# A decoder trunk on one core: query projection in 12 tiles instead of 16, with the rotary parts moved by DMA, and another order in front of the scan

## Chip, cores, metric

The kernel runs on one core of a Trainium2 chip. The metric is the device time of one execution in microseconds (us); lower is better. The engines are named as in the profile: PE (TensorE matrix products; PEld are its weight loads), DVE (VectorE), ACT (ScalarE), POOL (GpSimd), SP (SyncE, which issues most DMAs).

## What is computed

Two layers on 512 positions of width 1024, all in float32. Each layer has a mixer with two parallel head groups, then cross-attention into 256 memory tokens, then a gated MLP with a short convolution. The change is in the mixer:

```python
h = rmsnorm(x, norm_mix[i])
proj = h @ w_in[i]
z, xbc, dt_raw, c_q, c_kv, k_rope = jnp.split(proj, IN_SPLITS, axis=-1)
...
y = ssd_scan(xs, dt, a, bm, cm) + xs * d_skip[i][:, None]
...
q = (rmsnorm(c_q, q_norm) @ w_uq).reshape(b, s, MLA_HEADS, QK_NOPE + QK_ROPE)
q_nope = q[..., :QK_NOPE]
q_pe = apply_rope(q[..., QK_NOPE:], cos[:, :, None, :], sin[:, :, None, :])
kv = (rmsnorm(c_kv, kv_norm) @ w_ukv).reshape(b, s, MLA_HEADS, QK_NOPE + V_DIM)
...
k_pe = apply_rope(k_rope, cos, sin)
...
    sc = (jnp.einsum('bqhd,bkhd->bhqk', q_nope[:, q0:kend], k_nope[:, :kend])
          + jnp.einsum('bqhr,bkr->bhqk', q_pe[:, q0:kend], k_pe[:, :kend]))
```

There are 16 attention heads with 64 plain (nope) and 32 rotary (rope) query rows each; the query latent c_q has 384 channels, the key and value latent c_kv 256. The scan has 16 heads of 64 in 4 groups and runs over 4 chunks of 128 positions. `apply_rope` rotates pairs of rows by an angle that grows with the position.

## The kernel before

All matrices lie transposed: channels on the 128 partitions, the 512 positions along the free dimension. Every float32 product is made from three matmuls on values split into a high and a low part (`mm3`, L168 hi x hi, L169 hi x lo, L170 lo x hi). A result is split by `split`: ACT copies the high part (L159), DVE subtracts it for the low part (L162); with a scale it is L164 and L165. Weights come by DMA from SP into one of two raw buffers (L99, `fetch`), ACT makes the high part (L107) and POOL the low part (L108), each in three buffers; `weights` keeps two weights ahead. A raw buffer is free again when POOL has made the low part.

The order on PE is that of the program text (a manual schedule for PE alone). The other engines' instructions are put in order by a tile scheduler; each engine then runs its list strictly in order. `new("ps", ...)` takes one of 8 PSUM banks, `unit()` one of 68 SBUF tiles of 128x512.

A layer's mixer begins with the projections of the latents (`latent_q` three, `latent_kv` two), a projection that holds dt and the rotary keys, and the softplus chain for dt (L415 to L430). Then one loop runs the remaining projections (`inproj`, four groups of six tiles, each 24 matmuls of 128x512; four of a group pass a convolution over 4 positions on ACT and DVE: L485 scales the projection, L492, three times L494, a tanh in L495, the gate L496), and between the projections it hangs pieces of other work: the generator `front` from the first position on, and the four scans `ssd(g)` from the positions in START. Each `yield` gives way to the next projection:

```python
START = (5, 10, 16, 21)
...
for pos, _ in enumerate(chain(projections(), attention())):
    next(lead, None)
    ...
    for g in range(NG):
        if pos >= START[g]:
            next(scans[g], None)
```

`front` does, one piece at each position: the reciprocal root mean squares of the query latent (rq) and of the key latent (rk, and in layer 0 the rope tables, and the rotated keys kpe L440 to L443); the broadcast of rq and its products with the rope tables, csqa and csqb (L446, L447); the broadcast of rk and the normalised key latent (L452 and splits); the cumulative sums of dt x a by two matmuls (L460, L461) with acs, nacs, dtd and cd taken from them (L462 to L467); and the transposition of acs on PE (L470), which goes to DRAM and comes back broadcast (R in `ssd`).

A scan step `ssd(g)` transposes x, B and C pieces on PE (L515 to L522), makes xd = x dt and xdd = x dtd on DVE (L527, L536), exponentials on ACT (L543, L553) and their product with B x C on DVE (L554); after one more projection PE makes the states from xdd (L562), and later the outputs.

Attention goes head by head, in 16 steps. What a step holds is in strings: S scores of this head (`scores`: four blocks, on DVE a maximum L692, on ACT the exponential L695, the scale on POOL L697), K the keys of the next pair, V values, A outputs of two heads before (`attend`, L728 to L738), M one memory key tile (256 columns) in eight of the steps, T transposes of the head before (L709 and splits), Q the queries of two heads on (`queries`, L666):

```python
ORDER, FIRST, LAST = "SKVAMTQ", "VSKAMTQ", "SMAT"
```

A query tile is one head: 64 nope rows, 32 rope rows and the same 32 rope rows swapped, so that one multiplication with csqa (or csqb for odd heads, L666) gives the rotation's two products side by side; their sum is made inside the score product, since the keys hold kpe twice. 96 columns of weights thus cost a tile of 128, 16 tiles of nine matmuls per layer.

## Time and profile before

| | us |
|---|---|
| median of 3 runs | 1904.8 (1904.75 to 1904.96) |
| the profiled execution | 1904.88 |
| its span, from first to last instruction | 1903.2 |
| PE busy | 1867.0 (98%) |
| DVE, ACT, POOL busy | 1035.5, 950.2, 885.7 |
| granted clock of PE, mean | 0.995 |

Busy time is what an engine spends in instructions; idle time of an engine matters only where PE waits for it. The view of PE's waits sums such time by what ended it. The granted clock is given as a share of full speed: 1.0 is the 2.4 GHz level, 0.5 the 1.2 GHz level. Layer 0's front part runs from about 45 to 110 us and its attention from about 245 to 390 us; layer 1's from about 1000 and 1180 us.

### The profile page before, as it was taken

The page shows a single profiled execution, that of the slowest core. Times are in us where ns is not written, and L with a number is a line of the kernel's source. Part 1 is how long each engine was busy: PE and PEld are TensorE (multiplying, and loading weights), DVE is VectorE, ACT ScalarE, POOL GpSimd, SP SyncE. Part 2 cuts the span into 40 slices and gives each one's busy share as a digit, 9 for nine tenths or more (in the row PEclk, how much of TensorE's full clock was granted, in tenths as well). Part 3 has the DMA queues.
Part 4 walks back from the last instruction along what each step waited for, and adds up shares of the span by engine and source line. Part 5 has one row for each costly group of instructions (what it writes and reads, how often), then busy time and mean ns, then how long its engine had stood idle before and what let it go on. Part 6 is the DMA issues. An engine that isn't in the chain of part 4 may idle for free.

```text
span 1903.2 us, 24916 instructions
## 1 busy us (share of the span) xinstructions
PE 1867.0 (98%) x9264; PEld 1572.9 (83%) x9264; DVE 1035.5 (54%) x1967; ACT 950.2 (50%) x1694; POOL 885.7 (47%) x563
## 2 busy tenths in 40 slices
PE   8799999999999999999999999999999999999998
PEld 6588889988888888888887888898888888888887
DVE  5867788843343555541138777887334445555312
ACT  5366588843345444433235557888334544444321
POOL 5345455655416444433354454555553354444232
PEclk9899999999999999999999999999999999999999
DMA  5233311232213322233223332113322122332322
GB/s 168 68 122 111 103 51 59 93 125 94 91 34 109 100 100 97 92 97 100 92 100 101 113 110 82 58 62 122 110 91 88 50 96 98 100 100 90 102 91 84
DMA packets 56025, 178.47 MB, mean 94 GB/s; under 512 B 6368, under 2 KB 9312, under 8 KB 55904
## 3 DMA queue, kind: packets, MB, share of 16 engines
q1 hardware_dynamic: 49984, 166.32, 26.4%
q10 hardware_dynamic: 5920, 10.55, 1.7%
q8 instruction: 73, 1.20, 0.3%
q14 instruction: 48, 0.39, 0.1%
HBM read 174.69 MB, written 2.16 MB: 93 GB/s over the span
## 4 chain that ended last, share of the span: by engine, by line
PE 93%; DVE 2%; issue 1%; ACT 1%; POOL 1%; DMA 1%; SPq 0%; POOLq 0%; DVEq 0%; ACTq 0%
PE ps L168 28%; PE ps L170 28%; PE ps L169 28%; PE ps L728 2%; PE ps L709 1%; PE ps L583 1%; POOL wlo L108 1%; PE ps L589 1%; PE ps L562 1%; ACT whi L107 0%; DVE u L162 0%; PE ps L932 0%; PE ps L519 0%; PE ps L515 0%; PE ps L731 0%
## 5 line engine op out<-in xcount | busy, mean ns | idle before, releaser
L108 POOL TENSOR_TENSOR wlo<-wraw,whi 128x1024 fp32r<-128x1024 f32 (+1 forms) x290 | 679.1, 2343 | 855.7 <-ACT whi L107 836.6
L168 PE MATMUL ps<-u,whi 128*128 128x512 f32 (+1 forms) x2326 | 898.7, 386 | 7.7 <-ACT whi L107 5.1
L170 PE MATMUL ps<-u,wlo 128*128 128x512 f32 (+1 forms) x2326 | 890.0, 383 | 0.8 <-POOL wlo L108 0.6
L169 PE MATMUL ps<-u,whi 128*128 128x512 f32 (+1 forms) x2326 | 889.7, 383 | 0.0
L107 ACT ACTIVATE whi<-wraw 128x1024 fp32r<-128x1024 f32 (+2 forms) x319 | 328.2, 1030 | 494.7 <-PE ps L169 391.3
L168 PEld LDWEIGHTS ps<-u,whi 128*128 128x128 f32 x2326 | 438.9, 189 | 90.8 <-ACT whi L107 5.1
L170 PEld LDWEIGHTS ps<-u,wlo 128*128 128x128 f32 x2326 | 438.7, 189 | 87.3 <-POOL wlo L108 1.4
L169 PEld LDWEIGHTS ps<-u,whi 128*128 128x128 f32 x2326 | 439.2, 189 | 82.0 <-DVE u L165 0.7
L162 DVE TENSOR_TENSOR u<-ps,u 128x512 fp32r<-128x512 f32 (+2 forms) x236 | 137.2, 612 | 105.4 <-ACT u L159 104.7
L159 ACT ACTIVATE u<-ps 128x512 fp32r<-128x512 f32 (+2 forms) x236 | 117.7, 540 | 120.7 <-DVE ps L1021 98.4
L1017 DVE SCALAR_TENSOR_TENSOR u<-ps,small,u 128x510 f32<-128x510 f32 (+1 forms) x176 | 131.3, 749 | 74.7 <-ACT u L1015 71.7
L1010 DVE TENSOR_TENSOR ps<-ps,u 128x512 f32<-128x512 f32 x88 | 61.4, 700 | 109.9 <-PE ps L170 101.6
L301 POOL TENSOR_TENSOR u<-u,u 128x512 f32<-128x512 f32 (+1 forms) x82 | 102.5, 1251 | 37.0 <-ACT u L300 29.5
L108 DVE TENSOR_TENSOR wlo<-wraw,whi 128x1024 fp32r<-128x1024 f32 (+1 forms) x29 | 32.5, 1119 | 139.5 <-ACT whi L107 139.5
L697 POOL TENSOR_SCALAR u<-u,rs 128x512 f32<-128x512 f32 (+3 forms) x128 | 66.8, 537 | 79.7 <-DVE rs L696 75.0
L849 DVE TENSOR_TENSOR ps<-ps,u 128x512 f32<-128x512 f32 x32 | 22.4, 699 | 99.1 <-PE ps L170 99.1
L695 ACT ACTIVATE u<-ps,nm 128x512 f32<-128x512 f32 (+3 forms) x128 | 66.3, 524 | 18.1 <-DVE nm L692 12.1
L168 PE MATMUL ps<-u,u 128*128 128x512 f32 (+1 forms) x224 | 73.1, 326 | 0.9 <-ACT u L695 0.9
L170 PE MATMUL ps<-u,u 128*128 128x512 f32 (+1 forms) x224 | 72.1, 322 | 0.0
L169 PE MATMUL ps<-u,u 128*128 128x512 f32 (+1 forms) x224 | 72.0, 321 | 0.0
L494 DVE SCALAR_TENSOR_TENSOR u<-ps,half,u 128x509 f32<-128x509 f32 (+2 forms) x96 | 70.4, 742 | 1.2 <-ACT u L492 0.7
L1015 ACT ACTIVATE u<-ps,small 128x512 f32<-128x512 f32 x88 | 66.7, 760 | 1.7 <-DVE ps L1010 1.5
(193 smaller groups left out, 1769.3 us busy)
## 6 DMA issues: line engine op xcount, KB each, us to landing
wraw<-in_w_up SPq DMA_DIRECT2D x88, 512.0 KB, 3.4
wraw<-in_w_in SPq DMA_DIRECT2D x59, 512.0 KB, 3.5
wraw<-in_w_out SPq DMA_DIRECT2D x32, 512.0 KB, 3.4
wraw<-in_w_down SPq DMA_DIRECT2D x32, 512.0 KB, 3.4
u<-scr ACTq DMA_DIRECT2D x32, 256.0 KB, 4.6
wraw<-in_w_mk SPq DMA_DIRECT2D x16, 512.0 KB, 3.4
wraw<-in_w_mv SPq DMA_DIRECT2D x16, 512.0 KB, 3.4
wraw<-in_w_mq SPq DMA_DIRECT2D x16, 512.0 KB, 3.4
```

The lines of the kernel that those rows point to most:

```text
L107: A.activation(hi[:, c], raw[:, c], AF.Copy)
L108: eng.tensor_tensor(lo[:, c], raw[:, c], hi[:, c].bitcast(F32), ALU.subtract)
L159: A.activation(hi, src, AF.Copy)
L162: (leng or V).tensor_tensor(lo, src, hi.bitcast(F32), ALU.subtract)
L168: T.matmul(o, lh, rh, start=start, stop=False)
L169: T.matmul(o, lh, rl, start=False, stop=False)
L170: T.matmul(o, ll, rh, start=False, stop=stop)
L301: (eng or G).tensor_tensor(self.acc, self.acc, sq, ALU.add)
L494: V.scalar_tensor_tensor(r_[:, d:], acc[:, :S - d], cw(3 - d), r_[:, d:], ALU.mult, ALU.add)
L697: G.tensor_scalar(p_[:, :n], p_[:, :n], rs[:, i:i + 1], 1.0, ALU.mult, ALU.mult)
L1015: A.activation(y, acc, AF.Identity, scale=fw(2), bias=par(layer, "ffn_b", ch))
L1017: V.scalar_tensor_tensor(y[:, d:], acc[:, :S - d], fw(2 - d), y[:, d:], ALU.mult, ALU.add)
```

## The change

The weights of the queries are packed in 12 tiles per layer: four hold the rope rows of four heads each (`query_rope`), eight the nope rows of two heads each (`query_pair`). A rope tile is multiplied with the sine and with the cosine table into two banks, and both are split. The split rope rows (32 each) are then moved by DMA from SP into the query tiles of the heads, beside their nope rows: two products, high and low, two heads, so eight DMAs of 32x512 (64 KB) for each pair. The table of signs goes from the queries to the keys (`kro`, `krs`). The query latent is no longer multiplied in the query tile: `latent_q` keeps a copy, and `front` normalises and splits it (L482, L166 of the changed kernel).

In a step of attention the queries stand ahead of outputs and transposes, at the steps in UQ_AT. In `front`, the cumulative sums come one position earlier than the broadcasts; the rope tables and kpe follow behind the transposition of acs, then the key latent, then the query latent. The key tiles are filled one group later. The change's line numbers are those of the changed kernel, four to fourteen higher for the same statement in this part (L508 for L494, L499 for L485, L474 for L452, L541 for L527, L550 for L536, L576 for L562, L166 for L162).

```diff
+UQ = (-1, 0, 1, -1, 2, 3, -1, 4, 5, -1, 6, 7)
...
-    ORDER, FIRST, LAST = "SKVAMTQ", "VSKAMTQ", "SMAT"
+    ORDER, FIRST, LAST = "SKVMQAT", "VSKMQAT", "SMAT"
+    UQ_AT = (0, 1, 2, 4, 5, 6, 8, 9, 10, 12)
...
-        for nm, i, n in (("w_uv", 0, 1024), ("w_uk", 0, 1024), ("w_uq", 0, 768)):
+        for nm, i, n in (("w_uq", 0, 768), ("w_uv", 0, 1024), ("w_uk", 0, 1024)):
...
-            h_, l_ = unit(F32R), unit(F32R)
-            split(h_, l_, acc, par(layer, "q_norm", i))
+            r_ = unit()
+            A.copy(r_, acc)
             cqs.add(acc)
...
             rk = rstd_cols(cks.acc, KVL, rx)
-            if layer == 0:
-                rope_tables()
...
-            pq = bcast(rq)
-            V.tensor_tensor(csqa, pq, csa, ALU.mult)
-            V.tensor_tensor(csqb, pq, csb, ALU.mult)
-            yield
-            pk = bcast(rk)
...
+            yield
+            yield
             yield
 
             pa = bank()
...
             A.dma_start(scr, acsT)
+            yield
+
+            if layer == 0:
+                rope_tables()
...
+            kro, krs, ksh = unit(), unit(), unit()
...
+            yield
+            pk = bcast(rk)
...
+            yield
+            pq = bcast(rq)
+            for i in range(3):
+                V.scalar_tensor_tensor(cqr[i], cqr[i], par(layer, "q_norm", i), pq, ALU.mult, ALU.mult)
+                h_, l_ = unit(F32R), unit(F32R)
+                split(h_, l_, cqr[i])
...
+        def query_rope(i):
+
+            acc, sn = query_tile(i), bank()
+            V.tensor_tensor(sn, acc, css, ALU.mult)
+            V.tensor_tensor(acc, acc, csc, ALU.mult)
+            qpe[0] = []
+            for src in (acc, sn):
+                h_, l_ = unit(F32R), unit(F32R)
+                split(h_, l_, src)
+                qpe[0].append((h_, l_))
+
+        def query_pair(i, pr):
+
+            acc = query_tile(i)
+            for j in range(2):
+                qh, ql = unit(F32R), unit(F32R)
+                rows, r0, s0 = slice(64 * j, 64 * j + 64), 64 - 64 * j, 32 * ((2 * pr + j) % 4)
+                A.activation(qh[rows], acc[rows], AF.Copy)
+                V.tensor_tensor(ql[rows], acc[rows], qh[rows].bitcast(F32), ALU.subtract)
+                for c in range(2):
+                    for dst, src in zip((qh, ql), qpe[0][c]):
+                        nc.sync.dma_start(dst[r0 + 32 * c:r0 + 32 * c + 32].bitcast(F32),
+                                          src[s0:s0 + 32].bitcast(F32))
+                qq[2 * pr + j] = qh, ql
...
-                if g == 0:
+                if g == 1:
                     key_tiles()
```

Three places show how the order moves. **First place:** DVE around the products of the first scan step. In layer 0 before, ps_841 and ps_842 are the transposed x, u_866 and u_867 its xdd, ps_915 is the projection that PE finishes just ahead of the states matmul L562:

```order
L485 TENSOR_TENSOR ps_808<-ps_808,u_387 128x512
L527 TENSOR_TENSOR u_860<-ps_841,dt_151 128x512
L527 TENSOR_TENSOR u_862<-ps_842,dt_151 128x512
L494 SCALAR_TENSOR_TENSOR u_833<-ps_808,half,u_833 128x511
L536 TENSOR_TENSOR u_866<-ps_841,dtd_154 128x256
L494 SCALAR_TENSOR_TENSOR u_833<-ps_808,half,u_833 128x510
L536 TENSOR_TENSOR u_866<-ps_841,dtd_154 128x256
L494 SCALAR_TENSOR_TENSOR u_833<-ps_808,half,u_833 128x509
L536 TENSOR_TENSOR u_867<-ps_842,dtd_154 128x256
L485 TENSOR_TENSOR ps_915<-ps_915,u_387 128x512
```

In layer 0 of the change, ps_888 is the projection that PE finishes one broadcast (ps_921, of rq) ahead of the states matmul L576. The list begins

```order
L499 TENSOR_TENSOR ps_888<-ps_888,u_381 128x512
L482 SCALAR_TENSOR_TENSOR u_202<-u_202,small,ps_921 128x512
L482 SCALAR_TENSOR_TENSOR u_264<-u_264,small,ps_921 128x512
L474 SCALAR_TENSOR_TENSOR u_802<-u_336,small,ps_797 128x512
L508 SCALAR_TENSOR_TENSOR u_789<-ps_764,half,u_789 128x511
L482 SCALAR_TENSOR_TENSOR u_300<-u_300,small,ps_921 128x512
```

and after four more rows (L508, L166, L508, L474) ends with the gate, a low part, the products xd and, as u_839 and u_840, xdd:

```order
L510 SCALAR_TENSOR_TENSOR u_789<-ps_764,u_789 128x512
L166 TENSOR_TENSOR u_811<-u_808,u_810 128x512
L541 TENSOR_TENSOR u_833<-ps_814,dt_153 128x512
L541 TENSOR_TENSOR u_835<-ps_815,dt_153 128x512
L550 TENSOR_TENSOR u_839<-ps_814,dtd_156 128x256 x2
L550 TENSOR_TENSOR u_840<-ps_815,dtd_156 128x256
```

In layer 1 of the change (u_9131, u_9132 are xdd, ps_9180 is the projection ahead of the states matmul):

```order
L541 TENSOR_TENSOR u_9127<-ps_9107,dt_8499 128x512
L550 TENSOR_TENSOR u_9131<-ps_9106,dtd_8502 128x256 x2
L550 TENSOR_TENSOR u_9132<-ps_9107,dtd_8502 128x256
L499 TENSOR_TENSOR ps_9180<-ps_9180,u_8690 128x512
L482 SCALAR_TENSOR_TENSOR u_8538<-u_8538,small,ps_9213 128x512
```

The scaling of the projection ahead of the states matmul stood behind the three xdd before and does so in layer 1 of the change; in layer 0 of the change it stands ahead of them, with normalisations and splits between.

**Second place:** DVE in layer 0 around acs, before:

```order
L485 TENSOR_TENSOR ps_666<-ps_666,u_387 128x512
L162 TENSOR_TENSOR u_657<-u_654,u_656 128x512
L462 COPY acs_152<-ps_699 128x64
L463 TENSOR_SCALAR nacs_153<-ps_699 128x64
L494 SCALAR_TENSOR_TENSOR u_691<-ps_666,half,u_691 128x511
```

and of the change, where ps_609 is the projection just ahead of the two matmuls that fill ps_642:

```order
L510 SCALAR_TENSOR_TENSOR u_595<-ps_570,u_595 128x512
L499 TENSOR_TENSOR ps_609<-ps_609,u_381 128x512
L442 COPY acs_154<-ps_642 128x64
L443 TENSOR_SCALAR nacs_155<-ps_642 128x64
L444 TENSOR_TENSOR dtd_156<-ps_642,acs_154 128x64
```

The rows of the rope tables, of kpe, csqa and csqb and of the key latent that stood ahead of acs now stand behind it.

**Third place:** SP in layer 0's attention (u_2872 to u_2877 are split rope rows, u_2981 to u_2990 the query tiles of a pair). Before there were only weights:

```order
L99 DMA wraw_2961<-in_w_mk 128x1024
L99 DMA wraw_3022<-in_w_uq 128x768
L99 DMA wraw_3053<-in_w_mk 128x1024
L99 DMA wraw_3212<-in_w_uq 128x768
L99 DMA wraw_3298<-in_w_mk 128x1024
```

and of the change:

```order
L103 DMA wraw_3212<-in_w_uq 128x768
L704 DMA u_2981<-u_2872 32x512
L704 DMA u_2982<-u_2873 32x512
L704 DMA u_2981<-u_2876 32x512
L704 DMA u_2982<-u_2877 32x512
L704 DMA u_2989<-u_2872 32x512
L704 DMA u_2990<-u_2873 32x512
L704 DMA u_2989<-u_2876 32x512
L704 DMA u_2990<-u_2877 32x512
L103 DMA wraw_3333<-in_w_mk 128x1024
```

The eight DMAs of a pair stand between weight loads, behind one that waits for its raw buffer. On PE, 8780 rows become 8708; on SP, 332 become 456.

## Rows read from the trace of the kernel before

**Rows 1.** The page, part 1: busy us (share of the span), instructions.
```profile
PE 1867.0 (98%) x9264; PEld 1572.9 (83%) x9264; DVE 1035.5 (54%) x1967; ACT 950.2 (50%) x1694; POOL 885.7 (47%) x563
```

**Rows 2.** PE's waits: us in total, times, longest us.
```profile
PE ps L470 <- DVE acs L462: 10.7, 1, 10.7
PE ps L282 <- DVE rstd L275: 5.4, 2, 2.9
...
PE ps L168 <- ACT u L695: 1.9, 4, 0.5
```

**Rows 3.** PE's timeline in the fronts: start us, us, instruction [idle before <-releaser].
```profile
88.19 0.42 PE L470 MATMUL ps<-ident,acs 128*64 128x128 f32 x1 [10.67 <-DVE acs L462]
...
104.74 0.39 PE L168 MATMUL ps<-u,whi 128*128 128x512 f32 x1
...
107.91 0.39 PE L170 MATMUL ps<-u,wlo 128*128 128x512 f32 x1
108.14 1.46 PE L562 MATMUL ps<-u,u 128*128 128x256 f32 x6
...
1011.52 0.62 PE L282 MATMUL ps<-ident,rstd 128*128 128x128 f32 x4 [2.95 <-DVE rstd L275]
```

**Rows 4.** Windows: us, PE, PEld, DVE, ACT, POOL busy, granted clock, DMA share, GB/s.
```profile
260.00:360.00 100.00, 100.00 (x648) 91.94 (x647) 81.84 (x237) 83.76 (x205) 61.25 (x65) 1.00 0.20 65
...
280.00:300.00 20.00, 20.00 (x136) 18.53 (x135) 16.30 (x49) 17.54 (x45) 13.00 (x15) 1.00 0.24 74
...
88.20:91.00 2.80, 2.80 (x8) 2.22 (x9) 2.80 (x7) 0.97 (x3) 0.00 (x0) 0.50 0.61 187
...
1011.60:1019.00 7.40, 7.40 (x28) 6.02 (x29) 6.43 (x12) 3.66 (x5) 1.63 (x1) 0.77 0.20 71
```

**Rows 5.** DVE's timeline, layer 0's front.
```profile
84.53 0.69 DVE L496 SCALAR_TENSOR_TENSOR u<-ps,u 128x512 f32<-128x512 f32 x1
85.13 0.69 DVE L485 TENSOR_TENSOR ps<-ps,u 128x512 f32<-128x512 f32 x1
85.73 2.27 DVE L162 TENSOR_TENSOR u<-u,u 128x512 fp32r<-128x512 f32 x1
...
101.96 1.29 DVE L527 TENSOR_TENSOR u<-ps,dt 128x512 f32<-128x512 f32 x2
103.17 0.74 DVE L494 SCALAR_TENSOR_TENSOR u<-ps,half,u 128x511 f32<-128x511 f32 x1
103.83 0.41 DVE L536 TENSOR_TENSOR u<-ps,dtd 128x256 f32<-128x256 f32 x1
```

**Rows 6.** ACT's timeline, layer 0's front.
```profile
80.08 1.28 ACT L495 ACT_TABLE_LOAD   x1 [1.56 <-DVE u L494]
```

**Rows 7.** POOL's timeline, layer 0's front.
```profile
85.10 2.35 POOL L108 TENSOR_TENSOR wlo<-wraw,whi 128x1024 fp32r<-128x1024 f32 x1 [4.15 <-ACT whi L107]
```

**Rows 8.** PE's timeline, two steps of attention: first query matmul, outputs, first query matmul.
```profile
290.27 0.47 PE L168 MATMUL ps<-u,whi 128*128 128x512 f32 x1
...
304.98 0.98 PE L728 MATMUL ps<-u,u 128*128 128x512 f32 x4
...
307.28 0.48 PE L168 MATMUL ps<-u,whi 128*128 128x512 f32 x1
```

**Rows 9.** ACT's groups by shape, 260 to 360 us: busy us, mean ns of one.
```profile
L107 ACT ACTIVATE whi<-wraw 128x1024 fp32r<-128x1024 f32 x9 | 9.6, 1066 | 0.6 <-PE ps L169 0.4
...
L652 ACT ACTIVATE u<-ps 64x512 fp32r<-64x512 f32 x12 | 7.1, 590 | 1.9 <-PE ps L170 1.7
```

**Rows 10.** DMA issues: KB each, median us from issue to landing.
```profile
wraw<-in_w_uq SPq DMA_DIRECT2D x16, 384.0 KB, 3.1
...
out<-xall SPq DMA_DIRECT2D x8, 256.0 KB, 2.2
...
scr<-acsT ACTq DMA_DIRECT2D x2, 32.0 KB, 1.8
```

**Rows 11.** SP's timeline in attention: an issue.
```profile
267.94 0.33 SPq L99 DMA_DIRECT2D wraw<-in_w_uq  x1
```

125 lines of the change are left out of this document (66 added, 59 removed).

## The prediction, written before any run of the changed kernel

> **What bounds the kernel now.** I read the share of busy time first: TensorE (PE) is busy 98% of a span of 1903.2 us, every other engine about half [rows 1]. So only two things can shorten the run: fewer matmuls, or less of the little time in which PE waits. The windows then tell where PE has no gap: in the attention stretch from 260 to 360 us it is busy 100.00 of 100 us, with ACT at 83.76 and DVE at 81.84 [rows 4]. A matmul taken out there is worth its full issue time as long as ACT and DVE follow. The list of PE's waits shows the rest: 10.7 us once for the cumulative sums acs, 5.4 us in two waits for rstd in front of a broadcast, 1.9 us in four waits for the exponentials of the scores [rows 2]. The timeline puts the 10.67 us wait at 88.19, in layer 0's front part, and the longer of the two for rstd at 1011.52, in layer 1's [rows 3]. Behind such a wait the clock falls: the granted clock is 0.50 (the 1.2 GHz level) from 88.2 to 91.0 us, 1.4 us lost against the full level, and 0.77 over 7.4 us behind the wait at 1011.5, 1.7 us lost [rows 4]. So the fronts lose 5.4 + 10.7 + 1.4 + 1.7 = 19.2 us: 14.6 in layer 0 (2.5 + 10.7 + 1.4), 4.6 in layer 1 (2.9 + 1.7).
>
> **The sum** is made against the profiled execution, 1904.88 us, of which 1.7 us lie outside its span; the median of the runs is 1904.8, so nothing has to be converted. A measurement of this kernel can tell about 0.2%, 3.8 us, from no change.
>
> **1. Query tiles.** 12 tiles of nine 128x512 matmuls replace 16, in both layers: 2 x 4 x 9 = 72 fewer, and PE gets nothing new (8780 rows become 8708). From the one that starts at 104.74 to the one at 107.91 are 14 steps, 0.2264 us each [rows 3]. 72 x 0.2264 = **-16.3 us**, at full value because PE has no gap where they stood [rows 4].
>
> **2. Layer 0's front.** The acs sums leave the place behind the rope tables and the two csq products on DVE (second place shown). They now stand directly behind the scaling of the projection just ahead, and the transposition that needs them (L450) has 24 matmuls, 24 x 0.2264 = 5.4 us, in front of it. The 10.7 us wait goes to about nothing, and so does the 2.5 us wait, since the rq broadcast comes four positions later.
>
> What is late next is the scan's first step. Its states matmul (L576, L562 before) needs the products xdd. Before, DVE had xdd done at 103.83 + about 2.4, the matmul came at 108.14 and waited for nothing [rows 3, 5]. Now xdd stands behind a row that scales the projection PE has just finished, and behind 11 more (first place): DVE can begin the lot only when PE is one broadcast away from L576. Worked out by the distance from start to start in the DVE timeline [rows 5]: the scaling 0.60, like L485; three normalisations of the query latent and two of the key latent at 0.66, the distance behind L494, which is the same kind of instruction, 3.3; three convolution steps, L494 itself, 2.0; the gate 0.60; two low parts at 0.60, 1.2; two products xd 1.2; three xdd at 0.41 or less, 1.1. Sum 10.0. Inside it DVE waits for a tanh on ACT, which first loads its table since a sine ran before: 1.28 [rows 6] and a pass over 512 columns, 0.59 [rows 9], less one DVE operation of 0.66 that runs meanwhile, 1.2 and a handover of 0.1: 11.3. The rope chain before it, six 32-row operations with two ACT copies between, ends by my count about 0.5 us after PE is ready, and the broadcast takes 0.4 off: **a new wait of about 11.4 us**, and the clock falls again, 1.4. Loss 12.8 against 14.6: **-1.8**. The bounds: 9.6 without table and rope chain (-3.6), and 14 with one collision on top (+0.8).
>
> That collision is seen in one row: the low part at 85.73 took 2.27 us instead of 0.60, beside a POOL operation of 2.35 us that began at 85.10 [rows 5, 7]. Only two rows of my 11.4 read two tensors from SBUF, so I leave it to the upper bound. The Trainium skill, SBUF — State Buffer, section "Who interferes with whom", has this as an exclusive lock that a tensor_tensor with both inputs in SBUF meets when GpSimd reads; the row agrees. By that rule each low part could cost 1.7 us more and the wait would be up to 14.8 instead of 11.4.
>
> **3. Layer 1's front.** No rope tables there, and the xdd rows stand ahead of the scaling (first place, layer 1): DVE needs 8.0 us from the earlier scaling to the last xdd (10.0 less three normalisations), PE takes 5.4 for a projection and about 2 for transposes and a broadcast: a wait of 0 to 2. The 2.9 us wait goes; a collision like the one above can leave 2 at L450. I take 2.7 of loss against 4.6: **-1.9** (0 to -4.6; the lower clock comes back or not with the wait's length).
>
> **4. Attention.** DVE's work is the same: two multiplications less in each pair of tiles, as many splits more. ACT gets, per layer, 8 full splits (four rope tiles, two each) and 16 halves of 64 rows for 16 full splits, so eight passes over 512 columns more, at 0.59 each +4.7 us [rows 9], less two weight copies. Sixteen steps took 8 x 17.0 = 136 us [rows 8], of which ACT worked 84%, 114; now about 118 of 128, 92%. No stretch here shows ACT that full, and steps without a query tile alternate with longer ones, so some waits like those for the exponentials (0.5 at most before) must come. Between nothing and the 88% of a stretch where ACT had most to do, 280 to 300 us [rows 4] (118 / 0.88 = 134, +6), I take **+2 per layer, +4**.
>
> The rope DMAs: eight of 64 KB per pair of heads, 128 in all, on SP. None of that kind was there. Nearest rows: 1.8 us for 32 KB and 2.2 us for 256 KB out of SBUF, 3.1 us for 384 KB into it [rows 10]; an issue is 0.33 [rows 11]. I take 2.2, nearest in direction, between 1.8 and 3.1. They stand on SP behind a weight load that waits for a free buffer (third place), hence for the copy (1.07) [rows 9] and the low part (2.35) [rows 7] of another weight. Chain for the first head: 1.07 + 2.35 + 0.33 + 4 x 0.33 + 2.2 = 7.3, and 8.2 with 3.1. The time given: from the tile's first matmul its own 2.0, outputs and transposes 2.3 [rows 8], a whole step of about 8: 12.3. So **0**, hidden by five us; with POOL's and ACT's queues late by that, the scores wait.
>
> Sum: 1904.9 - 16.3 - 1.8 - 1.9 + 4 = **1888.9, say 1889 us**, from a lower end of 1904.9 - 16.3 - 3.6 - 4.6 + 0 = 1880 to an upper one of 1904.9 - 16.3 + 0.8 + 0 + 12 = 1901.
>
> **Rivals.** *The fronts come clean.* If DVE is ahead of PE at L576 after all, 19.2 us return nearly whole: 1904.9 - 16.3 - 17 + 2 = 1874. For it: a scaling that waits less, as in layer 1. Against: the rows run in order and the scaling can't begin before the last matmul. Between it and the forecast a half wait gives 1880.
>
> *ACT bounds attention.* With 12 instead of 4: 1897. For it: 92%. Against: the new order puts outputs and transposes last in a step, which gives their splits more room.
>
> *The rope DMAs follow one another* (slower). If a pair's eight transfers land one by one, its first head has 1.07 + 2.35 + 0.33 + 4t against 12.3: it waits once t is over 2.1. Each of 16 pairs then costs 4t - 8.6; the gain of 16.0 is used up at 1.0 a pair, t = 2.4; at t = 2.5 it is 1.4 x 16 = 22 us, 1904.9 - 16.0 + 22 = 1911. For it: 2.2 is near. Against: weight loads of this queue overlap, and DMA engines are busy 20% [rows 4].
> The Trainium skill, SBUF — State Buffer, section "Can I just issue two DMAs to hit both halves?", says that two at a time serialize, and "The DMA setup-cost knee" gives 64 KiB 138 GB/s, an estimate of 0.5 us apiece; by that eight take 4 us and fit, by its fixed 2 us each they would not. No row here shows which.
>
> *No change:* the freed 16 us are returned as waits in attention, ACT-bound with late transfers: 1901 to 1908.
>
> **Chances.** Forecast (1884 to 1894) 0.60; fronts clean or half (1872 to 1884) 0.14; ACT-bound (1894 to 1901) 0.16; no change 0.05; slower 0.05. Hence faster 0.90, same 0.05, slower 0.05. The range leaves out the cleanest fronts and the cases over 1901: 1878 to 1901.
>
> **What would show it.** Right: PE's matmul count 72 lower; no wait for acs near 88; a wait of about 11 us at L576 for DVE's L550 near 93 us with the clock at 0.5 behind it, and none over 2 in layer 1; PE waits in attention of a few us, for ACT; DMAs of about 2 us that nobody waits for. Wrong: PE waiting at the first matmul of the scores for a DMA queue, no wait at L576, or ACT over 95% with waits of 10 us a layer.

## The result, and the profile after

The changed kernel is slower: 1954.33 us (median of five runs, 1948.6 to 1956.37) against 1904.96 us for the kernel before in the same runs. The ratio is 1.0248, 95% interval 1.0237 to 1.0259, or +49.4 us. The forecast was 1889.0, range 1878 to 1901: wrong in sign and outside the range. The profiled execution of the changed kernel took 1956.37 us with a span of 1954.7, 51.5 us longer than the span before. It lies 2.0 us above the median; the five runs spread over 7.8 us.

The page of the changed kernel: busy time, the chain that ended last, and the transfers of the rope parts (KB each, median us from issue to landing).

```profile
PE 1875.8 (96%) x9192; PEld 1572.3 (80%) x9192; DVE 1049.4 (54%) x1967; ACT 958.1 (49%) x1712; POOL 880.0 (45%) x558
...
PE 82%; DVE 9%; ACT 3%; issue 2%; DMA 1%; POOL 1%; SPq 0%; POOLq 0%; ACTq 0%; DVEq 0%
...
u<-u SPq DMA_DIRECT2D x128, 64.0 KB, 2.2
```

The 72 matmuls are gone (9264 to 9192, [rows 1]) and DVE and ACT have only 14 and 8 us more to do. Yet PE's busy time rose by 8.8 us: fewer matmuls, more of them at the lower clock. A rope transfer lands 2.2 us after its issue, the value that the forecast took (the median of 128; they lie between 1.9 and 4.9).

PE's waits in the changed kernel (us in total, times, longest us):

```profile
PE ps L172 <- DVE u L701: 22.1, 12, 2.1
PE ps L576 <- DVE u L550: 18.0, 2, 13.8
...
PE ps L172 <- DVE u L647: 4.4, 6, 1.5
PE ps L754 <- ACT u L740: 4.3, 2, 2.2
PE ps L603 <- DVE u L587: 3.0, 4, 1.0
PE ps L603 <- ACT u L585: 2.8, 4, 1.1
PE ps L174 <- POOL wlo L112: 2.6, 3, 2.0
PE ps L450 <- DVE acs L442: 2.1, 2, 1.8
```

The 10.7 us for acs and the 5.4 us for rstd [rows 2] are gone, all but 2.1 us of acs. In their place stand two new lines at the head. (The 5.2 us for a weight's high part, left out here, are the start of the kernel; they were 5.1 before.) L576 is the wait that the forecast named: the states matmul of the first scan step waits for xdd (L550). L701 is one that it did not name: it is the subtraction that makes the low parts of a query pair, and the L172 that waits for it is the first matmul of the next keys, which reads nothing that L701 wrote. No line names a DMA.

Windows of the changed kernel (us; PE, PEld, DVE, ACT, POOL busy; granted clock; DMA share; GB/s), to be read against [rows 4]:

```profile
260.00:360.00 100.00, 86.89 (x517) 77.22 (x518) 76.19 (x217) 75.07 (x188) 46.43 (x55) 0.93 0.27 76
100.00:120.00 20.00, 9.26 (x30) 7.47 (x31) 12.65 (x21) 13.69 (x30) 4.91 (x5) 0.66 0.18 62
260.00:280.00 20.00, 14.52 (x63) 11.88 (x64) 15.26 (x46) 13.49 (x37) 6.82 (x10) 0.74 0.24 73
```

In 260 to 360 us PE was busy 100.00 of 100 us before and is busy 86.89 now, at a mean clock of 0.93 instead of 1.00. No engine is full: DVE 76, ACT 75. This is a stretch of short mutual waits, not one with a bottleneck engine. Behind some of the new waits the granted clock is nearer to its 1.2 GHz level: 0.66 around the wait in the front, 0.74 at the beginning of attention, where transposes and scores wait 2.11, 0.69 and 1.08 us within 6 us (L754, L754, L172), before the first wait for L701. Behind the later waits for L701, 1.57 to 1.93 us each in layer 0, it is 1.00 (300 to 360 us).

Where the 51.5 us of span are, from the starts in PE's timeline of the last states matmul of the scans (216.53 before, 227.41 now), of the last transposes of attention (371.42 and 399.52), and the same marks in layer 1:

| stretch | before | after | difference |
|---|---|---|---|
| to the last states matmul, layer 0 | 216.5 | 227.4 | +10.9 |
| attention, layer 0 | 154.9 | 172.1 | +17.2 |
| to the transposition of acs, layer 1 | 653.6 | 649.7 | -3.9 |
| front and scans, layer 1 | 126.6 | 138.4 | +11.9 |
| attention, layer 1 | 154.9 | 169.7 | +14.9 |
| the rest | 596.8 | 597.3 | +0.5 |

Some 60% of the loss (32.1 us) is in attention, where the forecast expected a gain of 6 us a layer. In layer 1 some 1 us of the -3.9 is only moved: the two broadcasts (0.60 us each) stood ahead of the transposition of acs and now stand behind it, while the sums and the transposition have kept their positions between the projections.

**The wait in attention.** Timelines of DVE and ACT in the changed kernel around one of the twelve waits (start us, us, instruction, idle before it and its releaser), and the waiting matmul in PE's:

```profile
273.98 0.58 ACT L700 ACTIVATE u<-ps 64x512 fp32r<-64x512 f32 x1
276.15 0.70 DVE L737 CUSTOM_DVE_ANT_0 ps<-ps,mask 128x512 f32<-128x512 f32 x1 [2.57 <-PE ps L174]
276.84 0.55 DVE L737 CUSTOM_DVE_ANT_0 ps<-ps,mask 128x384 f32<-128x384 f32 x1
277.31 0.68 DVE L701 TENSOR_TENSOR u<-ps,u 64x512 fp32r<-64x512 f32 x1
278.02 0.59 ACT L700 ACTIVATE u<-ps 64x512 fp32r<-64x512 f32 x1 [3.46 <-DVE u L701]
278.64 0.69 DVE L701 TENSOR_TENSOR u<-ps,u 64x512 fp32r<-64x512 f32 x1 [0.26 <-ACT u L700]
279.37 0.68 DVE L783 TENSOR_TENSOR u<-ps,u 64x512 f32<-64x512 f32 x1
279.48 0.47 PE L172 MATMUL ps<-u,whi 128*128 128x512 f32 x1 [2.12 <-DVE u L701]
```

The high part of the pair's first head is ready at 274.56 (273.98 + 0.58). DVE does nothing for 2.57 us before 276.15, because the next instruction in its list is a maximum (L737) over scores that PE is still computing. Only then come the first low part, the second high part on ACT, and the second low part, 278.64 to 279.33; the keys start at 279.48. The program hands out PSUM banks in a ring of eight, and the keys' bank is the one that the query pair held eight allocations earlier (three for this step's scores, three transposes, the outputs, the pair). With queries at the end of a step, the eighth allocation back is the outputs'.

**The fronts.** DVE, POOL and PE in the changed kernel, layer 0 and layer 1:

```profile
99.54 0.70 DVE L499 TENSOR_TENSOR ps<-ps,u 128x512 f32<-128x512 f32 x1
...
107.78 0.69 DVE L510 SCALAR_TENSOR_TENSOR u<-ps,u 128x512 f32<-128x512 f32 x1 [1.35 <-ACT ps L509]
...
110.18 1.08 DVE L550 TENSOR_TENSOR u<-ps,dtd 128x256 f32<-128x256 f32 x3
110.74 2.90 PE L576 MATMUL ps<-u,u 128*128 128x256 f32 x6 [13.76 <-DVE u L550]
...
121.58 2.66 DVE L166 TENSOR_TENSOR u<-u,u 128x512 fp32r<-128x512 f32 x1
...
1065.86 2.40 POOL L112 TENSOR_TENSOR wlo<-wraw,whi 128x1024 fp32r<-128x1024 f32 x1 [6.19 <-ACT whi L111]
1066.33 2.47 DVE L166 TENSOR_TENSOR u<-u,u 128x512 fp32r<-128x512 f32 x1
...
1073.18 2.05 PE L576 MATMUL ps<-u,u 128*128 128x256 f32 x4 [4.28 <-DVE u L550]
```

PE has nothing to do from 96.98 (110.74 - 13.76). DVE reaches the scaling L499 at 99.54, 2.6 us later, and the first xdd lets PE go at 110.74, 11.2 us after that. In layer 1 a low part with both inputs in SBUF takes 2.47 us beside a POOL operation of 2.40 that began 0.5 us earlier; its neighbour at 1070.81 takes 0.69. That is the collision of [rows 5, 7], and the Trainium skill, SBUF — State Buffer, section "Who interferes with whom", states it as a rule; the rows agree. The change has more of such work than its DVE total shows: the normalised query latent is split from SBUF, so the two fronts have ten low parts with both inputs in SBUF (12.2 us) where there were four (4.8 us). Three of the ten took 2.06 to 2.66 us, among them the one at 121.58, in the list ahead of the second scan step's waits at L603.

### The profile page after: what moved, and what is told of

It reads as the page before. It is cut to its first block, busy times and chain, and to the rows that moved or that the text cites. A ratio compares the mean times of both kernels' runs of the same rounds, so it can differ in the third digit from the quotient of the medians.

```text
span 1954.7 us, 25186 instructions
## 1 busy us (share of the span) xinstructions
PE 1875.8 (96%) x9192; PEld 1572.3 (80%) x9192; DVE 1049.4 (54%) x1967; ACT 958.1 (49%) x1712; POOL 880.0 (45%) x558
## 4 chain that ended last, share of the span: by engine, by line
PE 82%; DVE 9%; ACT 3%; issue 2%; DMA 1%; POOL 1%; SPq 0%; POOLq 0%; ACTq 0%; DVEq 0%
PE ps L172 26%; PE ps L174 26%; PE ps L173 25%; DVE u L508 1%; PE ps L773 1%; PE ps L754 1%; DVE ps L737 1%; DVE u L701 1%; DVE u L166 1%; POOL wlo L112 1%; PE ps L576 1%; ACT u L740 1%; DVE ps L499 1%; ACT whi L111 0%; DMA wraw<-in_w_in 0%
## 5 line engine op out<-in xcount | busy, mean ns | idle before, releaser
L172 PE MATMUL ps<-u,whi 128*128 128x512 f32 (+1 forms) x2302 | 892.2, 388 | 28.0 <-DVE u L701 22.1
L174 PE MATMUL ps<-u,wlo 128*128 128x512 f32 (+1 forms) x2302 | 884.8, 384 | 3.1 <-POOL wlo L112 2.6
L172 PEld LDWEIGHTS ps<-u,whi 128*128 128x128 f32 x2302 | 437.4, 190 | 114.1 <-issue 24.2
L174 PEld LDWEIGHTS ps<-u,wlo 128*128 128x128 f32 x2302 | 436.8, 190 | 89.8 <-POOL wlo L112 3.9
L166 DVE TENSOR_TENSOR u<-ps,u 128x512 fp32r<-128x512 f32 (+2 forms) x220 | 126.5, 607 | 103.9 <-ACT u L163 102.0
L163 ACT ACTIVATE u<-ps 128x512 fp32r<-128x512 f32 (+2 forms) x220 | 108.6, 535 | 119.8 <-DVE ps L1069 98.4
L172 PE MATMUL ps<-u,u 128*128 128x512 f32 (+1 forms) x224 | 77.0, 344 | 5.4 <-DVE u L647 3.9
L173 PE MATMUL ps<-u,u 128*128 128x512 f32 (+1 forms) x224 | 73.1, 326 | 0.0
L508 DVE SCALAR_TENSOR_TENSOR u<-ps,half,u 128x509 f32<-128x509 f32 (+2 forms) x96 | 69.8, 743 | 5.6 <-ACT u L506 4.5
L174 PE MATMUL ps<-u,u 128*128 128x512 f32 (+1 forms) x224 | 72.8, 325 | 0.0
```

The lines of the kernel that those rows point to most:

```text
L163: A.activation(hi, src, AF.Copy)
L166: (leng or V).tensor_tensor(lo, src, hi.bitcast(F32), ALU.subtract)
L172: T.matmul(o, lh, rh, start=start, stop=False)
L173: T.matmul(o, lh, rl, start=False, stop=False)
L174: T.matmul(o, ll, rh, start=False, stop=stop)
L508: V.scalar_tensor_tensor(r_[:, d:], acc[:, :S - d], cw(3 - d), r_[:, d:], ALU.mult, ALU.add)
```

## The experiments

All ratios are against the kernel before on the same chip, where its median lay between 1904.96 and 1906.24 us. "Attention" is the stretch of the table above, layer 0 and layer 1 (before: 154.9 and 154.9; the changed kernel: 172.1 and 169.7).

### Is it the place of the queries in a step, and is it the front?

**Queries last** (in the changed kernel):

```diff
-    ORDER, FIRST, LAST = "SKVMQAT", "VSKMQAT", "SMAT"
+    ORDER, FIRST, LAST = "SKVAMTQ", "VSKAMTQ", "SMAT"
```

> The changed kernel with the queries at the end of a step again (order S K V A M T Q), all else as changed. Theory 1 (bank): the keys of an odd step take the PSUM bank that the query pair of the step before held, eight allocations earlier, and PE waits until DVE has made its second low part; with the queries last the eighth allocation before the keys is the outputs' bank, so the 12 waits for the low parts (22 us) and the half clock behind them (about 6 us) go: 1915 to 1930 us. Theory 2 (rope DMAs late): the waits stay with the scores, since each pair then has less time until its use: 1950 or more. Theory 3 (ACT too full): the waits move to other places of the steps: 1945 to 1960.

Measured: 1935.89 us, 1.0163 [1.0148, 1.0179]; attention 162.0 and 161.8. PE's waits in this kernel:

```profile
PE ps L576 <- DVE u L550: 18.1, 2, 13.8
PE ps L773 <- DVE u L166: 7.2, 8, 1.5
```

The keys' 22.1 us of waits for L701 are gone, and 18.4 us with them: the place of the queries was worth that. But less came back than expected: attention is still 7 us a layer longer than before, and a smaller wait has grown from 0.6 to 7.2 us, the outputs (L773) for the low part of the transposes (L166).

**Front pieces later** (in the changed kernel, behind the DMA of acs):

```diff
             A.dma_start(scr, acsT)
             yield
+            yield
+            yield
+            yield
```

> The changed kernel with the rope tables, the key latent and the query latent three positions later in the front part, so that the products xdd of the first scan step stand ahead of them on DVE. If DVE's list ahead of xdd is what the states matmul waits for, the waits of 13.8 and 4.3 us go, with 12 matmuls at half clock (2.7 us): about 1934 us, 1930 to 1940. Rival: the same DVE work makes a later wait in front of the second scan step or of the keys, and the time stays at 1945 to 1956.

Measured: 1954.84 us, 1.0266 [1.0239, 1.0293]. PE's timeline in layer 0 (x runs are cut where a wait stands):

```profile
125.39 0.63 PE L532 MATMUL ps<-ident,u 128*128 128x128 f32 x4 [1.83 <-DVE u L485]
131.40 1.11 PE L532 MATMUL ps<-ident,u 128*128 128x128 f32 x4 [5.38 <-DVE u L607]
134.75 2.08 PE L536 MATMUL ps<-u,u 128*128 128x128 f32 x8 [2.24 <-DVE u L513]
146.07 1.53 PE L579 MATMUL ps<-u,u 128*128 128x256 f32 x6 [3.00 <-DVE u L553]
```

The 13.8 us wait in the first scan step is gone, and 12.45 us of waits stand in the second. It is the amount of DVE work in this part that PE waits for; moved, it is late somewhere else.

**Both moves together**, queries last and the three yields:

> Queries last in a step and the front part's late pieces three positions later, together. If the two losses are independent, both savings add: 1895 to 1910 us, with about 3 us left that the start loses (third weight tile late on POOL). Rival: the queries last make the attention wait elsewhere: 1910 to 1930.

Measured: 1936.55 us, 1.0162 [1.0147, 1.0177], the same as with queries last alone. A miss, for the reason just named.

**The old front and the old order, with twelve tiles.** The edit is the first one and, in `front`, the pieces in the order of the kernel before: rope tables and kpe beside rk, then the broadcast of rq with the normalised query latent, that of rk, the sums, the transposition; key tiles filled in group 0.

```diff
             rk = rstd_cols(cks.acc, KVL, rx)
-            yield
-            yield
-            yield
-            pa = bank()
...
+            if layer == 0:
+                rope_tables()
...
+            pq = bcast(rq)
...
             pk = bcast(rk)
...
+            pa = bank()
```

> Queries in 12 tiles with the rope DMAs, but the front part in the order of the kernel before (rope tables and rotated keys, query latent, key latent, then the cumulative sums) and the queries last in a step. If the front's new order and the queries cost independently, this loses only what attention lost in the run with queries last: 7.2 and 7.0 us a layer from the last scan's states to the last transposes, so about 1919 us (1915 to 1925). If the longer work on the query latent (three normalisations and splits in place of two products) was what made the new front slow, its cost comes back here ahead of the cumulative sums: 1930 or more.

Measured: 1919.36 us, 1.0078 [1.0063, 1.0093]; attention 161.4 and 160.8. So with twelve tiles the new front costs 16.5 us (1935.89 - 1919.36), and the twelve tiles alone, everything else in its old place, cost 14.1 us where 16.3 were to be gained.

**The new front alone**, in the kernel before with its sixteen tiles: the sums and the transposition ahead of the rope tables and broadcasts, key tiles in group 1.

```diff
             rk = rstd_cols(cks.acc, KVL, rx)
-            if layer == 0:
-                rope_tables()
...
+            yield
+            yield
+            yield
+            pa = bank()
...
+            if layer == 0:
+                rope_tables()
```

> The kernel before with nothing but the front part's new order (cumulative sums first, then rope tables and rotated keys, key latent, query broadcast; key tiles one group later); 16 query tiles as before. If the new order moves the same DVE work from a wait ahead of the sums into waits in the first two scan steps, the time gains nothing: 1905 to 1922 us. If the prediction's sum for the fronts holds (about 2 us saved in each layer), 1898 to 1903. The waits should be found at the first states matmul (about 10 us) and at the outputs' second matmul (1 to 2 us).

Measured: 1909.43 us, 1.0019 [1.0010, 1.0029]; attention 154.8 and 154.8. PE's timeline:

```profile
108.43 2.90 PE L566 MATMUL ps<-u,u 128*128 128x256 f32 x6 [14.28 <-DVE u L540]
```

The wait for acs has only changed its place, as in the changed kernel, and the kernel is 4 us slower. With sixteen tiles DVE has the two csq products in this place, with twelve three normalisations and three low parts: the parts of the change make each other worse. The new front costs 4.2 us with sixteen tiles and 16.5 with twelve. The way from the kernel before to the changed one is thus 14.1 (twelve tiles), 16.5 (the new front with them) and 18.4 us (the queries' place). That these add up to the loss shows nothing by itself, since each is the difference from one kernel to the next; in another order the pieces would have other sizes.

### What do the keys wait for?

**High parts first.** If the turns that ACT and DVE take with the two heads of a pair were the cost, then both high parts ahead of both low parts would free the bank sooner:

```diff
                 A.activation(qh[rows], acc[rows], AF.Copy)
-                V.tensor_tensor(ql[rows], acc[rows], qh[rows].bitcast(F32), ALU.subtract)
...
+            for j in range(2):
+                qh, ql = qq[2 * pr + j]
+                rows = slice(64 * j, 64 * j + 64)
+                V.tensor_tensor(ql[rows], acc[rows], qh[rows].bitcast(F32), ALU.subtract)
```

> The changed kernel with the two high parts of a query pair made one behind the other on ACT, and then the two low parts on DVE. In the changed kernel the second high part waits for the first low part (the two engines take turns on one bank). If these turns make the bank late, each of 12 waits becomes shorter by the DVE operation and its hand-over, 1 to 1.5 us: 1930 to 1942 us with the clock. If the bank is late because DVE stands in front of the next step's maxima, nothing changes: 1948 to 1956.

Measured: 1960.34 us, 1.0286 [1.0271, 1.0302], 6 us slower than the changed kernel, above the ranges of both theories. The keys' twelve waits sum to 21.1 us instead of 22.1. In the same step both high parts are done at 272.94, and DVE begins the two low parts at 275.53, behind the maxima of the next scores. The theory of the turns falls.

**The pair's bank freed early.** One copy by ACT takes the whole pair to SBUF; POOL makes the high parts from there and DVE the low parts, so that only the copy holds the bank:

```diff
             acc = query_tile(i)
+            raw = unit()
+            A.copy(raw, acc)
...
-                A.activation(qh[rows], acc[rows], AF.Copy)
-                V.tensor_tensor(ql[rows], acc[rows], qh[rows].bitcast(F32), ALU.subtract)
+                G.tensor_copy(qh[rows], raw[rows])
+                V.tensor_tensor(ql[rows], raw[rows], qh[rows].bitcast(F32), ALU.subtract)
```

> The changed kernel, order unchanged, but a query pair leaves its PSUM bank by one ACT copy to SBUF; high parts are then made by POOL and low parts by DVE from that copy. If the keys wait for the bank (theory 1), the 12 waits of 1.6 to 2.1 us at the keys' first matmul go, as ACT's copy ends some 3 us before the keys: 1925 to 1935 us. If they wait because ACT and DVE are behind with the whole head's work (theory 3), the waits move to the next place where a result is due, the outputs or the scores: 1945 to 1956.

Measured: 1951.9 us, 1.0246 [1.0231, 1.0262], hardly faster. Timelines of ACT, PE and DVE in this kernel, the same step:

```profile
269.81 0.58 ACT L698 COPY u<-ps 128x512 f32<-128x512 f32 x1
...
273.52 0.40 PE L172 MATMUL ps<-u,whi 128*128 128x512 f32 x1
...
276.21 0.68 DVE L785 TENSOR_TENSOR u<-ps,u 64x512 f32<-64x512 f32 x1
276.95 0.39 PE L172 MATMUL ps<-u,whi 128*128 128x256 f32 x1 [1.88 <-DVE u L785]
```

The copy is done at 270.39, and the keys start at 273.52 without a wait. Now the tile behind them, a memory key tile (128x256), waits 1.88 us for L785: the sum that frees the outputs' bank, which is the eighth allocation back from there and which DVE reaches behind the maxima and the same low parts. Twelve such waits sum to 19.4 us, where the keys' were 22.1. So it was the bank that held the keys, as supposed; but a freed bank only passes the wait on to the next tile in the ring, which DVE frees late as well. The rival, that ACT and DVE are behind altogether, gave the right time; whether the order of DVE's list or its amount makes it late here, this run doesn't tell.

### Why do twelve tiles lose, even in the old places?

**Steps evened out.** In the kernel with the old front, memory key tiles and queries in other steps:

```diff
-    MEM_AT = (3, 5, 7, 9, 11, 13, 14, 15)
+    MEM_AT = (4, 6, 8, 10, 12, 13, 14, 15)
...
-    UQ_AT = (0, 1, 2, 4, 5, 6, 8, 9, 10, 12)
+    UQ_AT = (0, 1, 2, 3, 5, 6, 7, 9, 10, 11)
```

> As the run with the old front, but with the attention's work dealt out evenly: memory keys mostly at steps without query tile or key tile (4, 6, 8, 10, 12 to 15), queries at 0 to 3, 5 to 7, 9 to 11, so that PE's step is 7.2 to 9.3 us and none is 4.7. Theory: in the run with queries last the steps without a query tile were shorter on PE (4.7 us) than ACT and DVE need for a head (about 7), so the removed matmuls came back as waits for the low parts of the transposes. Then this saves most of 16 us against the old front's run: 1903 to 1910 us. Rival: ACT's load over the whole stretch decides, not its spread: no change against that run.

Measured: 1919.69 us, 1.0079 [1.0064, 1.0094]: no change.

**Fewer matmuls and nothing else.** In the kernel before, with sixteen tiles, 12 of the 16 heads leave out the last 128 of the 384 latent channels:

```diff
-            for k in range(3):
+            n = 3 if h % 4 == 3 else 2
+            for k in range(n):
...
-                mm3(acc, uqh[:, o:o + P], uql[:, o:o + P], cqh[k], cql[k], k == 0, k == 2)
+                mm3(acc, uqh[:, o:o + P], uql[:, o:o + P], cqh[k], cql[k], k == 0, k == n - 1)
```

> The kernel before, with 36 query matmuls fewer in each layer and nothing else changed: 12 of the 16 heads leave out the last 128 of the 384 latent channels in their query tile (three matmuls each), so the queries are not the reference's. If a matmul taken out of attention is worth its issue time, as the prediction's first step says, this is 72 x 0.2264 = 16.3 us faster: about 1889 us. If ACT's and DVE's work on a head needs about the 8.5 us that a step has now, the time comes back as waits for the low parts and exponentials: 1897 to 1905.

Measured: 1899.09 us, 0.9963 [0.9949, 0.9977]; attention 151.5 and 151.4. Seventy-two matmuls are worth 7.1 us here (4.4 to 9.7 by the interval), 3.4 in each attention, not 16.3. The window of this kernel (columns as above):

```profile
260.00:360.00 100.00, 99.20 (x645) 90.25 (x645) 83.07 (x243) 86.29 (x213) 62.80 (x68) 1.00 0.21 69
```

PE is still busy 99.20 of 100 us, although it has less to do: the ends of matmuls in the profile are modelled, so a busy time need not show waits of one or two tenths of a microsecond between them. ACT rose from 83.76 to 86.29. This run measures what a freed PE is worth here.

**The same number, taken from one kind of step.** Counted from one head's transposes to the next head's, steps alternate in length: one with a memory key tile and a key tile, some 10.6 us, and one without, 6.4 to 6.8. (Queries stand behind the transposes, so those at the end of a step of the program with a memory key tile fall into the short step that follows.) I took 72 matmuls out of short steps alone, then out of long ones alone:

```diff
-            for k in range(3):
+            n = 1 if h in (3, 5, 7, 9, 11, 13) else 3
+            for k in range(n):
```

(for the long ones, heads 4, 6, 8, 10, 12, 14).

> The kernel before, with the last two latent channel blocks left out of the query product for six heads (3, 5, 7, 9, 11, 13): 36 matmuls fewer a layer, 72 in all, all of them in the steps that hold no memory key tile and take 6.4 to 6.8 us; the result of those heads is not the reference's. Theory (a floor of about 6.1 us for such a step): 0.3 to 0.6 us of the 1.36 us in each is gained, 12 times, so 1898 to 1902. Rival 1 (every matmul counts in full): 1889. Rival 2 (a uniform 43%, wherever it stands): 1898, as in the run with a quarter fewer.

> The kernel before, with the same 36 matmuls a layer left out for the heads 4, 6, 8, 10, 12 and 14, that is in the steps that hold a memory key tile and a key tile and take 10.6 us; the result of those heads is not the reference's. Theory (a long step has more matmuls in proportion to its chain, so its floor lies lower): most of 12 x 1.36 = 16.3 us comes back, 1890 to 1895, clearly less than with the short steps. Rival (a uniform 43%): 1898, the same as with the short steps.

Measured: short steps 1899.68 us, 0.9963 [0.9951, 0.9976], attention 150.8 and 151.2; long steps 1904.07 us, 0.9991 [0.9982, 0.9999], attention 153.1 and 154.0 (2.4 us of the total were lost ahead of layer 0's attention, where this kernel has the same instructions as the one before). The first total lies in the theory's range, but the theory falls, and with its sign reversed: short steps gave more. In the ten steps of the table below they came down to 5.5 to 5.8 us in four of five (6.1 in the last), below the floor of 6.1 that was supposed, and the long steps between them took 10.6 to 11.0 us instead of 10.6. PE's waits with lighter long steps, and its timeline:

```profile
PE ps L168 <- ACT u L696: 5.6, 12, 0.9
...
PE ps L168 <- DVE u L739: 3.1, 8, 0.4
...
293.57 0.39 PE L168 MATMUL ps<-u,u 128*128 128x256 f32 x1 [0.44 <-ACT u L696]
294.97 0.50 PE L168 MATMUL ps<-u,whi 128*128 128x512 f32 x1 [0.42 <-DVE u L739]
```

The scores of the long step come 1.4 us sooner and wait for the exponentials of the step before (L696), whose bank they take by the ring of eight; the keys then wait for the sum (L739) that frees the outputs' bank. In the kernel before the same two waits are 1.9 us in four [rows 2] and

```profile
PE ps L168 <- DVE u L738: 0.8, 2, 0.4
```

so with all its tiles it ran just behind these two results.

**Matmuls put back.** In the kernel with the old front, nine matmuls into a bank that nobody reads, in each of three steps without a query tile:

```diff
                     query_pair(i, UQ[i])
+            elif h in (3, 7, 11):
+                uqh, uql = uq[0]
+                acc = bank()
+                for k in range(3):
+                    o = k * P
+                    mm3(acc, uqh[:, o:o + P], uql[:, o:o + P], cqh[k], cql[k], k == 0, k == 2)
```

> The twelve-tile kernel with the old order and the old front pieces, and with 27 query matmuls a layer put back where none stand now: in steps 3, 7 and 11 nine matmuls of 128x512 go into a bank that nobody reads, after the transposes. Theory (a step with few matmuls is set by its chain through VectorE and ScalarE, 6 to 7 us, so that leaving out its nine query matmuls gave nothing back): no change within 4 us of the kernel without them, 1919 to 1923. Rival (TensorE bounds those steps and the time was lost elsewhere): 54 x 0.2264 = 12.2 us more, about 1931; with the 43% that the fewer-matmuls run showed, about 5 more, 1924.

Measured: 1923.82 us, 1.0095 [1.0079, 1.0110], 4.5 us more than without (4.0 against each run's own kernel before) for 12.2 us of matmuls; attention in the two profiles differs by 1.5 and 1.3 us. The time lies just above the theory's range and at the 43% of the rival, and doesn't tell them apart; but it shows what such steps are worth: from transposes to transposes, steps 3, 7 and 11 of layer 0 took 6.74, 6.96 and 6.98 us without query matmuls and 6.84, 6.64 and 7.83 with nine, 0.6 us more in all for 6.1 us of matmuls. In the kernel without them, PE's and DVE's timelines in step 3:

```profile
270.45 0.42 DVE L166 TENSOR_TENSOR u<-ps,u 128x256 fp32r<-128x256 f32 x1
...
271.60 0.55 DVE L732 CUSTOM_DVE_ANT_0 ps<-ps,mask 128x384 f32<-128x384 f32 x1
...
272.08 1.48 DVE L166 TENSOR_TENSOR u<-ps,u 128x512 fp32r<-128x512 f32 x3
272.81 0.91 PE L768 MATMUL ps<-u,u 128*128 128x512 f32 x3 [1.49 <-DVE u L166]
```

The outputs wait for the transposes' low parts, which stand in DVE's list between the maxima of a step that now follows sooner. The mean length of two steps (a long and a short one), over ten steps, from the third to the thirteenth transposes of layer 0, tells it in one table (layer 1 differs by at most 0.17):

| kernel | us for two steps | query matmuls in them, mean |
|---|---|---|
| before | 17.17 | 18 |
| a quarter of the query matmuls left out | 16.57 | 13.2 |
| lighter short steps | 16.51 | 12 |
| lighter long steps | 16.76 | 12 |
| twelve tiles, old order and front | 17.50 | 12.6 |
| the same, nine matmuls put back in three steps | 17.86 | 18 |

Some 16.5 us seem to be what the work of ACT and DVE allows for two heads, whatever PE has to do; the kernel before is only 0.7 us above. No run took work from ACT or DVE, so this is inferred. The twelve tiles, with as few matmuls as the lighter kernels, are 0.7 to 1.0 us above those. Their number of matmuls can't be the reason; what is left is the new queries' own work, a rope tile's two products and two splits, the pair's four half splits, in lumps of four a step or none, and the banks that these hold. That is argued from what the other runs leave over; none of it was tried by itself.

The ten steps are also not where most of the twelve tiles' loss lies. In layer 0 of the kernel with the old order and front, attention is 6.5 us longer than before (161.4 against 154.9), and 5.9 of these stand ahead of the third transposes, where PE has as many matmuls as before (271 in both profiles) and takes 54.36 us for them instead of 48.49. There the first transposes wait for DVE and then for an exponential,

```profile
246.49 0.44 PE L749 MATMUL ps<-ident,u 128*128 128x128 f32 x2 [1.82 <-ACT u L735]
```

and the granted clock is 0.73 from 245 to 250 us; the kernel before has no wait over 0.5 us in this part and a clock of 1.00. Layer 1 has the same, 4.5 of 5.9 us.

### Is there a better version?

**Rope tables early**, in the kernel before: their 10.7 us wait for acs comes from DVE being late with the tables, and they depend on nothing in the layer.

```diff
             prepare()
+            rope_tables()
...
-            if layer == 0:
-                rope_tables()
```

> The kernel before, with the rope tables of layer 0 computed some 20 us earlier, behind the projection that holds dt, where DVE is idle about half of the time; nothing else changed. If the 10.7 us wait for the cumulative sums is DVE's backlog with these tables in it (8 to 9 us of DVE), the wait shrinks to 2 to 4 us and the half clock behind it mostly goes: 1894 to 1899 us. If DVE is as full there, the wait moves to the dt chain: 1903 to 1906.

Measured: 1898.16 us, 0.9959 [0.9945, 0.9974], faster than both kernels. PE's waits, the head of the list:

```profile
PE ps L282 <- DVE rstd L275: 6.4, 2, 3.4
PE ps L168 <- ACT whi L107: 6.1, 1, 6.1
```

No line for acs is left; 8.1 us came back of 10.7. With the new front as well (the same edit in the run with the new front alone):

> The run with the front's new order alone, with the rope tables early as well. If that run's wait of 14.3 us at the first states matmul is the tables and rotated keys ahead of xdd on DVE, it shrinks by the tables' 8 to 9 us: 1897 to 1902 us. Rival: the scaling of the projection just ahead, and key latent and gate behind it, hold xdd alone: the wait stays over 9 us and the time over 1903.

Measured: 1899.89 us, 0.9968 [0.9957, 0.9979]. With the tables out of the way the new front gains nothing: 1.7 us behind the tables alone.

**A smoother front**: tables early, the sums one position sooner, then the key latent, the query broadcast last.

> The kernel before (16 tiles) with the rope tables early, and in the front part the cumulative sums and their transposition one position earlier than the broadcasts, key latent next, query broadcast last, so that DVE's list has no long run of rows that nobody needs yet. If the waits for rstd in front of the query broadcast (3.4 and 2.9 us in the run with the tables early) come from the broadcast standing one position behind its rstd, they go, and the half clock behind them: 1890 to 1895 us. If POOL's long operation beside rstd delays the sums instead: 1897 to 1900.

Measured: 1902.11 us, 0.9983 [0.9973, 0.9993], 4 us slower than the tables alone. PE's timeline:

```profile
70.11 0.69 PE L446 MATMUL ps<-dt,triu 128*128 128x64 f32 x2 [5.04 <-DVE dt L431]
```

The sums are now asked for before the softplus chain has made dt: 5.04 us here and 4.31 in layer 1.

**Tables early with twelve tiles** (old order, old front), and the same with the pair's bank freed early:

> The run with the old front and queries last, with the rope tables early and nothing else. 1911 to 1914 us if the tables are worth about 6 us there too; against the run with the bank freed early it tells what the freed bank is worth with the queries last: nothing if the keys then take the outputs' bank.

> 12 query tiles with the old front order, queries last, rope tables early, and the pair's bank freed by one ACT copy. Against the run with the old front (1919): the tables early save about 6 us as they did on the kernel before, the copy saves one ACT pass a pair (5 us of ACT a layer): 1908 to 1914 us. If ACT's and DVE's work for a head bounds attention, then 12 tiles do not come below the kernel before even so (1905); if PE did, 1895 to 1900.

Measured: 1920.96 us, 1.0087 [1.0072, 1.0102], and 1925.17 us, 1.0103 [1.0087, 1.0118]. Both are misses. In the first, layer 0's wait for acs has become one of 6.8 us for dt (L429), ahead of the sums; the second, with the high parts on POOL, is 4 us slower still.

## Why the prediction was wrong, step by step

**Step 1, the query tiles: -16.3 us "at full value because PE has no gap where they stood".** This failed. The count of matmuls was right, its price was not: with everything else unchanged, 72 fewer gave 7.1 us, 43%. The working names the condition, "as long as ACT and DVE follow", and then took PE busy 100.00 of 100 us [rows 4] as proof that it holds. ACT at 84% and DVE at 82% were just behind, and took over after some 0.6 us per pair of steps: with lighter long steps PE waits 8.7 us for their results where it waited 2.7.

**Step 4, attention: +2 us a layer.** This is the step that failed most. Without the query tiles' 8.15 us a layer, 154.9 should have become 146.7 + 2; it became 172.1 and 169.7, so the term was +25 and +23. Its parts are measured. A layer's matmuls brought 3.4 instead of 8.15. The new queries in the old places made it 161.4 (+9.9 over the 151.5 of the fewer matmuls). The new front left attention 0.6 and 1.0 longer still (162.0 and 161.8). The queries ahead of outputs and transposes added 10.1 in layer 0 and 7.9 in layer 1 (172.1 against 162.0, 169.7 against 161.8), by a chain that the working didn't look for: the ring of banks, and a DVE list in which the next scores' maxima stand ahead of the low parts. I counted what ACT has to do (92% of the time) and not in which order and for whom. In the profile no engine came near that share: ACT was at 75%.

**The rope transfers: 0.** Right for the changed kernel: 2.2 us each, as taken, and PE waits for none. An issue was mis-sized, 0.54 us (median of 128) instead of 0.33. With queries last there was one wait of 0.2 us for a transfer, with the old front too one of 0.8, with both moves together two of 1.5 us in sum. The rival of transfers one after the other, the only slower one, isn't what happened: a pair's eight are issued within 4.95 us, each landing some 2.2 us later, which eight times 2.2 in a row would not allow.

**Step 2, layer 0's front: a wait of 11.4 at L576, a loss of 12.8 against 14.6.** The place and the cause were right, the size nearly: 13.76 us. The list from the scaling to xdd took 11.2 us, against 11.3 forecast, which is in part luck: the 11.3 counts all three xdd (11.3 less 0.7 up to the first), and PE went on after the first. (The working says 11 rows between, where its sum has all 13; and the 2.5 us wait that went stood at the broadcast of rk, not of rq.) The mis-sized term is what comes ahead: rope tables and rope chain end 2.6 us after the broadcast, where the forecast had 0.1 (0.5 less 0.4). The clock behind the wait cost 2.6 us (0.64 over 7.26 us) instead of 1.4. What failed is the sum beside it. It assumed that after this wait the scan would run as before. Between the first states matmul (+2.6 against before) and the fourth (+10.9) another 8.3 us went: 3.0 in four waits of L603 for ACT and DVE, and 5.3 in which PE was busy longer with as many matmuls, at a mean granted clock of 0.96 instead of 1.00. At the very start PE loses 2.0 us at L174, and the clock is 0.91 from 20 to 40 us: the copy of the query latent, its square and eight squares of the input stand on ACT ahead of a weight's high part, which no step mentioned.

**Step 3, layer 1's front: a loss of 2.7 against 4.6.** Here the wait of "0 to 2" at L576 was 4.28 us. Two collisions stand ahead of it: a row of the rope chain (L462) took 2.05 us beside POOL where layer 0's took 0.75, and a low part 2.47 instead of 0.69; the working left collisions to its upper bound. The gain was real: the stretch up to acs shrank by 3.9, of which some 1 us is moved. But front and scans lengthened by 11.9.

**The rivals.** None of the four gives 1954. "No change" had the freed time returned as waits in attention, which is in part the right mechanism, and stopped where it was used up. Nothing in the list said that a reordering on PE can cost more than it saves, and none of the signs named for being wrong appeared: no wait at the scores for a DMA queue, a wait at L576, ACT far from 95%.

What stays open: which instructions of the new queries delay the beginning of attention and make two steps 1 us longer (14.1 us of the 49.4 hang on this), and how much of the 16.5 us for two heads is ACT's, how much DVE's order.

## What to carry to other kernels

A window in which PE is busy 100% is no proof that a matmul taken out is worth its time: with two engines at 82 and 84% behind it, each in order, 43% came back here. Before an edit frees time on the bound engine, leave the work out in a throwaway version and see what the others allow; that one run would have halved the forecast's gain. When an order of steps is changed, follow each PSUM bank to its next user: a tile can wait for a low part that it never reads, because an in-order engine has put the next step's work first.
